# Attention inside a hybrid encoder layer: v in groups of eight columns, and TensorE's transposes in longer runs

## The chip, the cores and the metric

The kernel runs on one core of one Trainium2 chip. The metric is the device time of one execution in microseconds (us). Before the change three runs gave a median of 1982.31 us (1982.19 to 1984.06).

## The reference

The layer works on 512 tokens of width 2048, which lie on a grid of 8 rows and 64 columns. All numbers are float32. One input projection is split between two groups. Group A is a convolution module with a LayerNorm. Group B is attention: 16 heads of 64 numbers, and each query sees all 8 rows and a window of 16 columns, clamped at the grid's edge. Both results are normalised, put side by side, projected, and added to x; a gated MLP with a short convolution and a last norm follow.

```python
proj = einsum("bsd,dc->bsc", rms_norm(x, attn_norm_g), w_in)   # u_val, u_gate, q, k, v
# attention, for a row r of the grid; col_idx[c] = 16 columns around c, clamped to the grid
k_win = k_rows[:, :, col_idx];  v_win = v_rows[:, :, col_idx]
scores = einsum("bchd,bicjhd->bchij", q_row * 64**-0.5, k_win) + bias     # rows i, columns j
p = softmax(scores over (i, j))
out = einsum("bchij,bicjhd->bchd", p, v_win)
# the rest of the layer
mixed = concat(rms_norm(y_conv), rms_norm(y_na))
x = x + mixed @ w_out
up = depthwise_conv(rms_norm(x) @ w_up, width 3);  gate, val = split(up)
x = x + (silu(gate) * val) @ w_down
return rms_norm(x)
```

## The kernel before, in words

**Matmuls of the weights.** Weights come in units of 128 x 1024 numbers. `parts` (L128) splits each into a high part `whi` on ScalarE (L131) and a low part `wlo` on VectorE (L132), and `group` (L144) runs 24 matmuls on it: eight pairs of high parts (L148 and L149) and then eight with the low part (L151). `weights` (L170) prepares three units ahead, and there are four buffers for each part. An input projection of 128 output columns is two units (`project`, L335). `ORDER` says which projections come when: "a" is group A's, "q" is q, k and v of a pair of heads.

**Attention in steps.** The sixteen heads are worked on as eight pairs. `qkv(p)` (L437) projects q, k and v of a pair, transposed, with the channels of the two heads on the 128 partitions and the 512 tokens along the free axis. `attend(p, ...)` (L459) is a generator. After every unit of weights `tick` (L156) lets the next step of the oldest unfinished generator be issued behind the unit's last matmul; a second list, `asteps`, does the same for group A's norms (`group_a`, L398), which begin with pair 5. Each `yield` is the end of a step. The steps of a pair are:

- load the two halves of the bias table, and transpose v (L467, tile `trv`, ScalarE's copies `vt` at L469);
- scores (L478, tile `sc`) of four blocks of 16 columns, each against 32 columns of keys, for both heads, and the softmax of each half (L488 to L496, tile `s`);
- one empty step;
- `turn` of the first half (L506, tile `trp`; ScalarE's copies `pt` at L511), eight transposes, a copy behind each four;
- `turn` of the second half;
- values (L520, tile `po`), and behind them the copy `ao` (L554) and its split.

Block b of the queries uses the columns from `KC0[b]` = 0, 8, 24, 32 on, 32 of them in 8 rows, so 256 keys. For v, `qkv` writes these four windows out, one behind the other (L454), and as they overlap, 1024 columns stand where there are 512 tokens. So v takes eight transposes of 128 x 128.

**PSUM.** Eight banks: three for projections (`mm`), two for the tag `sc`, two for `tr`, one for `po`. The scores and the probabilities' transposes use `sc` and `tr`, v's transposes `tr`, the values `po`, and the norms' sums (`stat`, L223) the first bank of `sc`. Both halves of a tile under `sc` are one tile to the scheduler.

**Order.** A scheduler orders each engine's instructions by priority and by its own estimate of when they are ready. `pin` (keep_in_program_order) ties an instruction of TensorE to the one issued before it. `shifted(-SOONER)` gives the copies `pt` an earlier priority. Behind the input projections comes `out_half` (L581): sixteen units with group A's part, which also still carry the last steps of attention, and sixteen with attention's part. All of the MLP follows it.

Of the kernel before, what the change touches and what calls it, by code (L numbers as in the profile page):

```python
# [10 lines left out]
F32 = mybir.dt.float32  # L11
F32R = mybir.dt.float32r
AF = mybir.ActivationFunctionType
# [3 lines left out]
P = 128  # L17
D = 2048
S = 512
GW = 64  # L20
CONV = 1024
HEADS = 16
DH = 64
NA = 1024
CK = 31
WH = 8
# [7 lines left out]
NF = FF // P  # L34
U = 8
PAD = CK // 2
KW = 32
BLK = 16
NB = GW // BLK
KC0 = [0, 8, 24, 32]  # L40
H = S // 2
NK = NF // 2
KEEP = 4
# [15 lines left out]
ROW = 2048  # L59
ORDER = "aaaqqaqaaaqqaqqq"  # L60
NORM_AT = 5
RA_AFTER = 5

PCOLS = [("g1", KD), ("dww", NC_ * CK), ("dwb", NC_), ("lng", NC_), ("lnb", NC_), ("cog", NC_),
# [10 lines left out]
def layer(ctx: ExitStack, tc: tile.TileContext, xT, xn, w_0, w_in, w_out, w_up, w_down, par, tab, g3, out):  # L75
    nc = tc.nc
# [6 lines left out]
    psa = ctx.enter_context(tc.tile_pool(name="psa", bufs=1, space=bass.MemoryType.PSUM))  # L83
# [9 lines left out]
    def t2(name, dt=F32):  # L93
        return tp.tile([P, S], dt, tag="t2k", name=name)
# [86 lines left out]
    sums = {}  # L181
# [48 lines left out]
    def root_steps(sums, n, name):  # L230
# [17 lines left out]
        ps = stat()  # L248
# [3 lines left out]
        nc.scalar.activation(res, ps, AF.Copy)  # L252
        return res

    def rsqrt_steps(acc, n, name):
# [4 lines left out]
        return (yield from root_steps(ps[:, :S // P], n, name))  # L260


    xs, x1 = [], []
    pin = tc.keep_in_program_order
# [33 lines left out]
    for u in range(2):  # L298
        raw, i = raw_unit(w_in[NC_ + 1, :, u * U * P:(u + 1) * U * P], U * P)
# [15 lines left out]
    for step in ORDER:  # L315
        i = next(a_ if step == "a" else q_)
# [7 lines left out]
    rstd, late = [], []  # L324
# [71 lines left out]
    ma, ra = [], []  # L396

    def group_a():  # L398
        yield
        while taps:  # L400
            yield
        acc = t2("acc")
        nc.vector.tensor_add(acc, ys[0], ys[1])
        for i in range(2, NC_):
            nc.vector.tensor_add(acc, acc, ys[i])
        yield
        ps = psa.tile([P, 2, S], F32, tag="sc", name="st")[:, 0]
        nc.tensor.matmul(ps, ones, acc, start=True, stop=True)
        mu = t2("mu")
        nc.vector.tensor_scalar(mu, ps, 1.0 / CONV, None, op0=ALU.mult)  # L410
        acc = t2("acc")
        for i in range(NC_):
            nc.vector.tensor_sub(ys[i], ys[i], mu)
            sum_sq(acc, ys[i], i == 0)
        yield
        yield
        r = yield from rsqrt_steps(acc, CONV, "rln")
        acc = t2("acc")
        for i in range(NC_):
            nc.vector.tensor_mul(ys[i], ys[i], r)  # L420
            nc.scalar.activation(ys[i], ys[i], AF.Silu, scale=pc("lng", i), bias=pc("lnb", i))
            ma.append(split(ys[i], pc("cog", i), "ma"))
        for i in range(NC_):
            sum_sq(acc, ys[i], i == 0)
        for _ in range(RA_AFTER):
            yield

        ra.append((yield from rsqrt_steps(acc, CONV, "ra")))


    mb, rb = [], []
# [2 lines left out]
    def grid(t, c0, w):  # L434
        return t.rearrange("p (r c) -> p r c", c=GW)[:, :, c0:c0 + w]

    def qkv(p):  # L437
        got = []
        for j, nm in enumerate("qkv"):
            ps = project(2 * NC_ + j * NP_ + p)  # L440
            if nm == "q":

                t = t2(nm)
                by = "p (r b c) -> p r b c"
                nc.vector.tensor_mul(t.rearrange("p (b r c) -> p r b c", b=NB, r=WH),
                                     ps.rearrange(by, b=NB, r=WH), rstd[0].rearrange(by, b=NB, r=WH))
            elif nm == "k":
                t = t2(nm)
                nc.vector.tensor_mul(t, ps, rstd[0])
            else:  # L450

                t = [t2("vw").rearrange("p (b k) -> p b k", b=2) for _ in range(NB // 2)]
                for b in range(NB):
                    nc.vector.tensor_mul(t[b // 2][:, b % 2].rearrange("p (r c) -> p r c", c=KW), grid(ps, KC0[b], KW),  # L454
                                         grid(rstd[0], KC0[b], KW))
            got.append(t)
        return got

    def attend(p, q, k, v):  # L459


        hps = [slice(j * DH, (j + 1) * DH) for j in range(2)]
        vt = []
        for half in range(2):
            ps = psa.tile([P, 4, P], F32, tag="tr", name="trv", bufs=2)
            for c in range(4):
                nc.tensor.transpose(ps[:, c, :], v[half][:, c // 2, c % 2 * P:(c % 2 + 1) * P], ident)  # L467
            t = t2("vt").rearrange("p (c k) -> p c k", c=4)
            nc.scalar.activation(t, ps, AF.Copy)  # L469
            vt.append(t)  # L470
        po = psa.tile([P, S], F32, tag="po", name="po")
        soft = []

        def scores(b0, both, more=False):
            for i in range(2):
                b = b0 + i
                for j, hp in enumerate(hps):
                    m = nc.tensor.matmul(both[j][:, i, :], q[hp, b * P:(b + 1) * P], grid(k, KC0[b], KW)[hp],  # L478
                                         start=True, stop=True)
                    if more or i or j:  # L480
                        pin(m)
# [19 lines left out]
        def turn(two, more=False):  # L501
            for j in range(2):
                s, ps = soft.pop(0), two[j]
                for i in range(2):
                    for ch in range(2):
                        m = nc.tensor.transpose(ps[:, 2 * i + ch, :], s[:, i, ch * P:(ch + 1) * P], ident)  # L506
                        if more or i or j or ch:
                            pin(m)
                pt = t2("pt").rearrange("p (c k) -> p c k", c=4)
                with shifted(-SOONER):  # L510
                    nc.scalar.activation(pt, ps, AF.Copy)  # L511
                pts.append(pt)

        def values(b0, more=False):
            for i in range(2):
                b = b0 + i
                for ch in range(2):
                    for j in (1, 0):
                        hp = hps[j]
                        m = nc.tensor.matmul(grid(po, b * BLK, BLK)[hp], vt[b // 2][:, 2 * (b % 2) + ch, hp],  # L520
                                             pts[b0 + j][:, 2 * i + ch, :], start=(ch == 0), stop=(ch == 1))
                        if more or (i, ch, j) != (0, 0, 1):
                            pin(m)
# [13 lines left out]
        both = psa.tile([P, 2, 2, 2 * P], F32, tag="sc", name="sc")  # L537
        both = [both[:, j] for j in range(2)]
        more = [psa.tile([P, 2, 2 * P], F32, tag="tr", name="sc", bufs=2) for _ in range(2)]
        scores(0, both)  # L540
        scores(2, more, True)
        softmax(both)
        softmax(more)
        yield
        yield
        both = psa.tile([P, 2, 4, P], F32, tag="sc", name="trp")
        turn([both[:, j] for j in range(2)])
        yield
# [508 lines left out]
```

## Time and profile before

| what | value |
|---|---|
| median of three runs | 1982.31 us |
| profiled execution | 1981.86 us |
| its span, first to last instruction | 1980.1 us |
| TensorE busy | 1965.8 us, 99% |
| VectorE busy | 1617.2 us, 82% |
| ScalarE busy | 1098.3 us, 55% |
| TensorE's granted clock, mean | 0.998 |

The profile comes from one execution. "PE" is TensorE, "DVE" VectorE, "ACT" ScalarE, "SPq" the queue of SyncE, which issues loads; "L148" is line 148 of the kernel. A row of the timeline has the start in us, the duration in us (of the whole group, where like instructions follow each other), the engine, the line, the operation, output <- input, shapes and the count (x8). What stands in brackets is how long the engine sat idle before it, and who ended that. Matmuls overlap in a pipeline, so the step from one start to the next counts, not the duration. A scores matmul leaves two records, a transpose one.

### The profile page before, as it was taken

To read this page: it belongs to the slowest core of one execution; us is meant where nothing else is said; L and a number is where in the kernel's file an instruction comes from. 1 tells how busy PE (TensorE), PEld (TensorE's weight loads), DVE (VectorE), ACT (ScalarE), POOL (GpSimd) and SP (SyncE) were. 2 spreads that over 40 slices of the span, in tenths; PEclk is the share of its full clock that TensorE was granted. 3 is DMA by queue.
4 is the path that set the end of the run, shared out by engine and by line. 5 is a ranking of instruction groups with operands and counts; after the bars stand their busy time and mean duration, and the time that the engine had idled before them with its cause. 6 is when DMAs were issued, how large, how long until landed. Compare 5 with 4: busy or idle time off the path is not lost.

```text
span 1980.1 us, 27714 instructions
## 1 busy us (share of the span) xinstructions
PE 1965.8 (99%) x10173; PEld 1668.0 (84%) x10173; DVE 1617.2 (82%) x2362; ACT 1098.3 (55%) x1726; POOL 226.0 (11%) x310
## 2 busy tenths in 40 slices
PE   9999999999999999999999999999999999999998
PEld 7888888888788888888888888888888888888886
DVE  5987688788557888988888898989898898886765
ACT  7244424438525676666666666666666644554654
POOL 0111111111001111111111111111110400000000
PEclk9999999999999999999999999999999999999999
DMA  9776776776858889999999999999986977666663
GB/s 368 191 194 179 185 184 184 187 186 186 271 149 202 218 225 271 242 271 242 269 243 267 260 246 264 249 268 245 271 221 184 366 249 230 221 216 194 192 197 122
DMA packets 141817, 450.98 MB, mean 228 GB/s; under 512 B 15088, under 2 KB 23536, under 8 KB 140272
## 3 DMA queue, kind: packets, MB, share of 16 engines
q1 hardware_dynamic: 88880, 293.46, 44.3%
q0 software_dynamic: 42624, 148.92, 35.3%
q10 hardware_dynamic: 10176, 6.83, 1.1%
q8 instruction: 80, 1.31, 0.3%
q14 instruction: 57, 0.47, 0.1%
HBM read 430.27 MB, written 111.15 MB: 273 GB/s over the span
## 4 chain that ended last, share of the span: by engine, by line
PE 93%; ACT 2%; DVE 2%; DMA 1%; issue 1%; ACTq 0%; SPq 0%; DVEq 0%
PE pu L728 43%; PE pd L867 21%; PE pj L151 6%; PE pj L148 6%; PE pj L149 6%; PE po L148 3%; PE po L151 3%; PE po L149 3%; PE po L520 1%; PE trp L506 1%; ACT s L496 1%; PE pj L364 1%; DMA x<-in_xT 1%; DVE s L488 1%; ACT s L493 0%
## 5 line engine op out<-in xcount | busy, mean ns | idle before, releaser
L131 ACT ACTIVATE whi<-raw 128x1024 fp32r<-128x1024 f32 x573 | 605.1, 1057 | 573.1 <-PE pj L149 176.1
L132 DVE TENSOR_TENSOR wlo<-raw,whi 128x1024 fp32r<-128x1024 f32 x573 | 699.5, 1221 | 235.5 <-ACT whi L131 192.1
L728 PE MATMUL pu<-xc,whi 128*128 128x512 f32 x2464 | 593.6, 391 | 0.0
L728 PEld LDWEIGHTS pu<-xc,whi 128*128 128x128 f32 x2464 | 451.4, 188 | 86.7 <-DVE xc L616 0.4
L728 PEld LDWEIGHTS pu<-xc,wlo 128*128 128x128 f32 x2464 | 319.2, 191 | 13.7
L728 PE MATMUL pu<-xc,wlo 128*128 128x256 f32 x2464 | 324.2, 283 | 0.0
L867 PE MATMUL pd<-whi,ho 128*128 128x512 f32 x1232 | 305.0, 389 | 0.0
L867 PEld LDWEIGHTS pd<-whi,ho 128*128 128x128 f32 x1232 | 231.1, 188 | 48.6 <-DVE vl L741 0.5
L148 PE MATMUL pj<-xh,whi 128*128 128x512 f32 x608 | 241.4, 397 | 0.0
L149 PE MATMUL pj<-xl,whi 128*128 128x512 f32 x608 | 237.4, 391 | 0.0
L390 DVE SCALAR_TENSOR_TENSOR y<-ch,prm,y 128x500 f32<-128x500 f32 (+14 forms) x240 | 177.2, 741 | 5.1
L867 PE MATMUL pd<-wlo,ho 128*128 128x512 f32 x616 | 165.1, 389 | 0.0
L151 PE MATMUL pj<-xh,wlo 128*128 128x512 f32 x608 | 151.0, 390 | 0.0
L148 PEld LDWEIGHTS pj<-xh,whi 128*128 128x128 f32 x608 | 114.2, 188 | 26.4 <-issue 3.4
L867 PEld LDWEIGHTS pd<-wlo,ho 128*128 128x128 f32 x616 | 115.6, 188 | 24.0
L151 PEld LDWEIGHTS pj<-xh,wlo 128*128 128x128 f32 x608 | 114.1, 188 | 23.6
L149 PEld LDWEIGHTS pj<-xl,whi 128*128 128x128 f32 x608 | 114.3, 188 | 23.0 <-issue 0.2
L737 ACT ACTIVATE pu<-pu 128x512 f32<-128x512 f32 x132 | 76.5, 580 | 93.2 <-PE pu L728 93.2
L677 POOL DMA_DIRECT2D raw<-in_w_up x88 | 78.0, 887 | 361.3 <-DVE wlo L132 154.1
L203 POOL DMA_DIRECT2D ws<-in_w_down x88 | 79.6, 904 | 299.4 <-DMA ws<-in_w_down 115.6
L200 POOL DMA_DIRECT2D ws<-ws x44 | 23.4, 531 | 321.6 <-PE pj L151 109.2
L200 POOL DMA_DIRECT2D ws<-in_w_down x44 | 23.1, 524 | 321.5 <-PE pj L151 178.1
(185 smaller groups left out, 1986.7 us busy)
## 6 DMA issues: line engine op xcount, KB each, us to landing
raw<-in_w_up SPq DMA_DIRECT2D x220, 512.0 KB, 5.9
ws<-in_w_down POOLq DMA_DIRECT2D x132, 512.0 KB, 6.1
raw<-in_w_up POOLq DMA_DIRECT2D x88, 512.0 KB, 7.3
raw<-ws SPq DMA_DIRECT2D x88, 512.0 KB, 3.7
raw<-in_w_in SPq DMA_DIRECT2D x76, 512.0 KB, 5.2
raw<-in_w_down SPq DMA_DIRECT2D x66, 512.0 KB, 3.9
ws<-ws POOLq DMA_DIRECT2D x44, 512.0 KB, 5.7
raw<-in_w_out SPq DMA_DIRECT2D x32, 512.0 KB, 5.0
```

The source lines that it names most:

```text
L131: i = nc.scalar.activation(hi[:, :n], raw[:, :n], AF.Copy)
L132: j = nc.vector.tensor_sub(lo[:, :n], raw[:, :n], hi[:, :n].bitcast(F32))
L148: nc.tensor.matmul(ps, hi, mh, start=first and k == 0, stop=False)
L149: nc.tensor.matmul(ps, hi, ml, start=False, stop=False)
L151: i = nc.tensor.matmul(ps, lo[:, wk * P:(wk + 1) * P], mh, start=False, stop=last and k == len(ws) - 1)
L200: behind(nc.gpsimd.dma_start(wsum[c][k], a), ins)
L203: nc.gpsimd.dma_start(wsum[c][k], w_down[k, {1: A21, 2: A11, 4: A11, 6: A12}[c]], accum_op=ALU.add, max_dma_last_dim=ROW)
L390: nc.vector.scalar_tensor_tensor(y[:, a:b], h[:, a + j - PAD:b + j - PAD], prm[:, o:o + 1], y[:, a:b], op0=ALU.mult, op1=ALU.add)
L677: nc.gpsimd.dma_start(a[c], w_up[f, q2], accum_op=ALU.add)
L728: i = nc.tensor.matmul(ps[:, :n], part[:, k * P:(k + 1) * P], comb[c][k][:, :n], start=j == 0 and not more, stop=j == 2 * U - 1, skip_grou ...
L737: nc.scalar.activation(to, ps, AF.Copy)
L867: m = nc.tensor.matmul(ps[i], h[:, o + t * P:o + (t + 1) * P], w[:, d], start=start and not more and kind == 0 and j == 0, stop=stop and k ...
```

## The change

Keys and values are kept in groups of eight columns: `qkv` writes k and v as eight groups, each of 8 rows by 8 columns (64 numbers), so two neighbouring groups are 128 numbers in one piece. A window of 32 columns is four groups. Windows 0 and 3 begin at an even group (0 and 4) and are read in place; windows 1 and 2 begin at an odd one (1 and 3). For them there is a second copy of the keys, `ks`, with the groups in the order 2, 1, 4, 3, 6, 5; ScalarE makes it with two copies of 128 x 192. `KEYS` says for every block which of the two it reads and from where, `WITHIN` in which order the groups stand there, and the bias table is laid out for that order on the host.

Now v has four transposes, into the bank `po`. ScalarE copies the result three times: whole, and for each half of the partitions (one group of a pair) three quarters, so that the groups stand in the same order as in `ks`. These transposes are issued in the step of the scores, in one pinned run with them.

All sixteen transposes of the probabilities go into one step and one run, into two banks of `sc` and two of `tr`, and the four copies `pt` are issued behind the last of them. Three steps lie from the scores to this turn, four in pairs 5 and 6 (`LATER`), and the values follow one step later. The broadcast of group A's last norm, `ra`, takes its bank from `po`.

```diff
-KW = 32
-KC0 = [0, 8, 24, 32]
+HG = 8
+KEYS = ((0, 0), (1, 0), (1, 1), (0, 2))
+WITHIN = ((0, 1, 2, 3), (1, 0, 3, 2))
+LATER = (5, 6)
...
-        ra.append((yield from rsqrt_steps(acc, CONV, "ra")))
+        ra.append((yield from rsqrt_steps(acc, CONV, "ra",
+                                          lambda: psa.tile([P, S], F32, tag="po", name="st"))))
...
-            elif nm == "k":
+            else:
                 t = t2(nm)
-                nc.vector.tensor_mul(t, ps, rstd[0])
-            else:
-                t = [t2("vw").rearrange("p (b k) -> p b k", b=2) for _ in range(NB // 2)]
-                for b in range(NB):
-                    nc.vector.tensor_mul(t[b // 2][:, b % 2].rearrange("p (r c) -> p r c", c=KW), grid(ps, KC0[b], KW),
-                                         grid(rstd[0], KC0[b], KW))
+                by = "p (r g c) -> p r g c"
+                nc.vector.tensor_mul(t.rearrange("p (g r c) -> p r g c", g=2 * NB, r=WH),
+                                     ps.rearrange(by, g=2 * NB, r=WH), rstd[0].rearrange(by, g=2 * NB, r=WH))
+            if nm == "k":
+                ks = t2("ks")
+                at = "p (n s k) -> p n s k"
+                for i, by in enumerate((slice(1, NB), slice(0, NB - 1))):
+                    nc.scalar.activation(ks.rearrange(at, s=2, k=DH)[:, :NB - 1, i], t.rearrange(at, s=2, k=DH)[:, by, i],
+                                         AF.Copy)
+                t = t, ks
...
-        vt = []
-        for half in range(2):
-            ps = psa.tile([P, 4, P], F32, tag="tr", name="trv", bufs=2)
-            for c in range(4):
-                nc.tensor.transpose(ps[:, c, :], v[half][:, c // 2, c % 2 * P:(c % 2 + 1) * P], ident)
-            t = t2("vt").rearrange("p (c k) -> p c k", c=4)
-            nc.scalar.activation(t, ps, AF.Copy)
-            vt.append(t)
-        po = psa.tile([P, S], F32, tag="po", name="po")
+        def turned_v():
+            ps = psa.tile([P, NB, P], F32, tag="po", name="trv")
+            for c in range(NB):
+                m = nc.tensor.transpose(ps[:, c, :], v[:, c * P:(c + 1) * P], ident)
+                if c:
+                    pin(m)
+            vt.extend(t2("vt").rearrange("p (c k) -> p c k", c=NB) for _ in range(2))
+            nc.scalar.activation(vt[0], ps, AF.Copy)
+            for hp, by in zip(hps, (slice(1, NB), slice(0, NB - 1))):
+                nc.scalar.activation(vt[1][hp, :NB - 1], ps[hp, by], AF.Copy)
...
-                    m = nc.tensor.matmul(both[j][:, i, :], q[hp, b * P:(b + 1) * P], grid(k, KC0[b], KW)[hp],
+                    m = nc.tensor.matmul(both[j][:, i, :], q[hp, b * P:(b + 1) * P],
+                                         ks[KEYS[b][0]][hp, KEYS[b][1] * P:][:, :2 * P],
                                          start=True, stop=True)
...
+        def turned_p(two):
+            for ps in two:
                 pt = t2("pt").rearrange("p (c k) -> p c k", c=4)
                 with shifted(-SOONER):
                     nc.scalar.activation(pt, ps, AF.Copy)
                 pts.append(pt)
...
-        scores(0, both)
+        turned_v()
+        scores(0, both, True)
         scores(2, more, True)
         softmax(both)
         softmax(more)
+        for _ in range(4 if p in LATER else 3):
+            yield
+        both = psa.tile([P, 2, 4, P], F32, tag="sc", name="trp")
+        both = [both[:, j] for j in range(2)]
+        more = [psa.tile([P, 4, P], F32, tag="tr", name="trp", bufs=2) for _ in range(2)]
+        turn(both)
+        turn(more, True)
+        turned_p(both + more)
         yield
-        yield
-        both = psa.tile([P, 2, 4, P], F32, tag="sc", name="trp")
-        turn([both[:, j] for j in range(2)])
-        yield
-        turn([psa.tile([P, 4, P], F32, tag="tr", name="trp", bufs=2) for _ in range(2)])
-        yield
-        values(0)
-        values(2, True)
+        po = psa.tile([P, S], F32, tag="po", name="po")
+        values(po, 0)
+        values(po, 2, True)
```

More of the change, by code (lines that the diff above doesn't have):

```diff
@@ L228, in layer, with root_steps @@
     where = []
-    def root_steps(sums, n, name):
+    def root_steps(sums, n, name, bank=None):
         v, r, y = (sm.tile([P, S // P], F32, tag="rs" + c, name="rs" + c) for c in "vry")
@@ L247, in root_steps @@
         yield
-        ps = stat()
+        ps = bank() if bank else stat()
         for i in range(2):
@@ L253, in root_steps, with rsqrt_steps @@
         return res
-    def rsqrt_steps(acc, n, name):
+    def rsqrt_steps(acc, n, name, bank=None):
         ps = stat()
@@ L259, in rsqrt_steps @@
             nc.tensor.matmul(ps[:, i:i + 1], acc[:, i * P:(i + 1) * P], ones[:, 0:1], start=True, stop=True)
-        return (yield from root_steps(ps[:, :S // P], n, name))
+        return (yield from root_steps(ps[:, :S // P], n, name, bank))
     xs, x1 = [], []
@@ L456, in qkv, with attend @@
+            if nm == "k":
[5 more added lines that the diff above has]
+                t = t, ks
             got.append(t)
         return got
[L459 removed]
+    def attend(p, q, ks, v):
         hps = [slice(j * DH, (j + 1) * DH) for j in range(2)]
[L463 to L472 removed]
+        vt, soft = [], []
+        def turned_v():
[8 more added lines that the diff above has]
+                nc.scalar.activation(vt[1][hp, :NB - 1], ps[hp, by], AF.Copy)
@@ L512, in turn, with values @@
                 pts.append(pt)
-        def values(b0, more=False):
+        def values(po, b0, more=False):
             for i in range(2):
@@ L519, in values @@
                         hp = hps[j]
-                        m = nc.tensor.matmul(grid(po, b * BLK, BLK)[hp], vt[b // 2][:, 2 * (b % 2) + ch, hp],
+                        m = nc.tensor.matmul(grid(po, b * BLK, BLK)[hp], vt[KEYS[b][0]][:, KEYS[b][1] + ch, hp],
                                              pts[b0 + j][:, 2 * i + ch, :], start=(ch == 0), stop=(ch == 1))
@@ L1035 @@
     qr, qc = np.divmod(np.arange(P), BLK)
-    kr, kc = np.divmod(np.arange(2 * P), KW)
+    kg, kr, kc = np.unravel_index(np.arange(2 * P), (NB, WH, HG))
     tab = np.full((HEADS, 3, P, 2 * P), NEG, rpb.dtype)
@@ L1039 @@
         c = b * BLK + qc[:, None]
-        k = KC0[b] + kc[None, :]
+        swapped, at = KEYS[b]
+        k = ((2 * at + swapped + np.array(WITHIN[swapped])[kg]) * HG + kc)[None, :]
         start = np.clip(c - WW // 2, 0, GW - WW)
```

## The prediction

> **What bounds the kernel now.** I read the page first: shares of busy time, the granted clock, the chain that ended last.
>
> ```profile
> PE 1965.8 (99%) x10173; PEld 1668.0 (84%) x10173; DVE 1617.2 (82%) x2362; ACT 1098.3 (55%) x1726; POOL 226.0 (11%) x310
> ...
> PEclk9999999999999999999999999999999999999999
> ...
> PE 93%; ACT 2%; DVE 2%; DMA 1%; issue 1%; ACTq 0%; SPq 0%; DVEq 0%
> ```
>
> TensorE is busy 99% of the span at full clock and is 93% of the chain. So an instruction less on TensorE, or a wait less, should come off the end, unless it opens a gap. Next I read TensorE's timeline where pairs of heads are worked on. A unit is 24 projection matmuls, and its last eight (L151) make one row; from one such row to the next is one unit with what is put in between.
>
> ```profile
> 104.55 1.98 PE L151 MATMUL pj<-xh,wlo 128*128 128x512 f32 x8
> ...
> 109.99 1.98 PE L151 MATMUL pj<-xh,wlo 128*128 128x512 f32 x8
> 111.81 1.03 PE L467 MATMUL trv<-ident,vw 128*128 128x128 f32 x8
> ...
> 116.34 1.98 PE L151 MATMUL pj<-xh,wlo 128*128 128x512 f32 x8
> 118.25 2.00 PE L478 MATMUL sc<-k,q 64*128 64x256 f32 x16
> ...
> 123.97 1.98 PE L151 MATMUL pj<-xh,wlo 128*128 128x512 f32 x8
> ...
> 169.52 1.98 PE L151 MATMUL pj<-xh,wlo 128*128 128x512 f32 x8
> 171.34 0.60 PE L506 MATMUL trp<-ident,s 128*128 128x128 f32 x4
> ...
> 172.71 0.60 PE L506 MATMUL trp<-ident,s 128*128 128x128 f32 x4
> ...
> 175.92 1.98 PE L151 MATMUL pj<-xh,wlo 128*128 128x512 f32 x8
> 177.74 1.03 PE L506 MATMUL trp<-ident,s 128*128 128x128 f32 x8
> ...
> 182.27 1.97 PE L151 MATMUL pj<-xh,wlo 128*128 128x512 f32 x8
> 184.17 1.97 PE L520 MATMUL po<-pt,vt 128*64 128x128 f32 x32
> ...
> 189.83 1.98 PE L151 MATMUL pj<-xh,wlo 128*128 128x512 f32 x8
> ...
> 460.50 1.98 PE L151 MATMUL pj<-xh,wlo 128*128 128x512 f32 x8
> ...
> 544.90 1.98 PE L151 MATMUL po<-mah,wlo 128*128 128x512 f32 x8
> ...
> 551.29 1.98 PE L151 MATMUL po<-mah,wlo 128*128 128x512 f32 x8
> ...
> 557.24 1.98 PE L151 MATMUL po<-mah,wlo 128*128 128x512 f32 x8
> ```
>
> A unit with nothing in it takes 109.99 - 104.55 = 5.44 us. What a unit takes beyond 5.44 is the price of what was put in, drains and waits included: eight transposes of v 6.35 - 5.44 = 0.91; the scores 7.63 - 5.44 = 2.19; two runs of four transposes of the probabilities 6.40 - 5.44 = 0.96, so 0.48 a run; a run of eight 6.35 - 5.44 = 0.91; the values 7.56 - 5.44 = 2.12. From 4 to 8 transposes is 0.43, so one costs 0.107 and a run 0.05 on top.
>
> The whole stretch, by groups of instructions between its first and last row:
>
> ```profile
> L151 PE MATMUL pj<-xh,wlo 128*128 128x512 f32 x496 | 123.3, 390 | 0.0
> ...
> L151 PE MATMUL po<-mah,wlo 128*128 128x512 f32 x64 | 15.8, 389 | 0.0
> ```
>
> 560 such matmuls are 70 units, 380.8 us. From 109.99 to 557.24 are 447.25, so 66.45 us were put in. Of these the three norms, which the change only moves, take about 5.3: each 0.95 for its sums (544.90 to 551.29) and 0.5 for its broadcast (551.29 to 557.24), and some 0.95 for the mean's matmul, which I put at the price of the sums. Attention costs 61.1 us, 7.6 a pair, where the prices above make 0.91 + 2.19 + 0.96 + 0.91 + 2.12 = 7.09. The rest is waits:
>
> ```profile
> 129.41 1.98 PE L151 MATMUL pj<-xh,wlo 128*128 128x512 f32 x8
> ...
> 132.93 0.66 PE L506 MATMUL trp<-ident,s 128*128 128x128 f32 x4 [0.16 <-ACT pt L511]
> 136.19 1.98 PE L151 MATMUL pj<-xh,wlo 128*128 128x512 f32 x8
> ...
> 518.01 2.00 PE L478 MATMUL sc<-k,q 64*128 64x256 f32 x16 [0.79 <-ACT ra L252]
> ```
>
> In the first pair the two runs of four cost 6.78 - 5.44 = 1.34: the second waits for ScalarE's copy of the first, since both write one tile. Pairs 6 and 7 (counted from 0), which share the engines with group A's norms, are worst: 460.50 to 544.90 is 84.40 us for 12 units (65.28), so 19.12 put in, 17.2 without norms.
>
> **The change, part by part.**
>
> *v's transposes.* Four for eight, 32 fewer in all, in one run ahead of the scores. Four cost 0.43 to 0.48 by the rows above, depending on whether the run's 0.05 is shared with the scores. I take 0.45, so v and scores make 2.64 where they made 3.10. The scores' matmuls keep number and shape, and a keys' operand that lies in one piece of 256 columns, not eight of 32, I give no gain: 16 in 1.92 us is 0.12 for 256 columns, in proportion with the projections' 5.44/24 = 0.227 for 512. The scores start at 118.25, 0.10 behind the eight L151 that began at 116.34 (8 x 0.227 = 1.81). [...]
>
> *The probabilities' transposes.* Sixteen in one run: 16 x 0.107 + 0.05 = 1.77, where two runs of four and one of eight took 1.87 without waits and 2.2 with them. All four copies come behind, so no transpose waits for a copy.
>
> *The values.* Unchanged, 2.12. A pair now costs 2.64 + 1.77 + 2.12 = 6.53, eight 52.2.
>
> *ScalarE and VectorE.*
>
> ```profile
> L454 DVE TENSOR_TENSOR vw<-pj,rstd x32: 410/415/425, 106.6 to 506.7; 128x256 f32<-128x256 f32 x32
> ...
> L445 DVE TENSOR_TENSOR q<-pj,rstd x8: 679/682/691, 85.7 to 490.2; 128x512 f32<-128x512 f32 x8
> ...
> L469 ACT ACTIVATE vt<-trv x16: 576/596/599, 112.4 to 516.9; 128x512 f32<-128x512 f32 x16
> ...
> 130.55 0.90 ACT L496 ACTIVATE s<-s,su 128x256 f32<-128x256 f32 x2
> ...
> 110.19 1.06 ACT L131 ACTIVATE whi<-raw 128x1024 fp32r<-128x1024 f32 x1 [4.38 <-PE pj L149]
> ```
>
> VectorE's four multiplies for v (4 x 0.415) become one like q's (0.68; at worst the old 1.66), and k's stays one. ScalarE gets two copies of 128x192 for the shifted keys (nearest row: two of 128x256 in 0.90, so 0.5 to 0.9 together) and three copies of v for two (0.596 each; the two of 64x384 between 0.45 and 0.6): 0.8 to 1.5 us a pair more. ScalarE waits 4.38 us a unit for TensorE to give a weight buffer back, and that covers it. Without that cover, in pairs 5 to 7, the weights are still split some three units (16 us) ahead. I cost both at nothing.
>
> *Turn and values one tick apart.* The turn moves behind three units, not two, and for pairs 5 and 6 behind four; values stay a tick behind it, at the place of before for pairs 0 to 4 and 7. The scores at 118.25 had their last scaled probability at 130.55 + 0.90 = 131.45; the turn came at 129.41 + 1.81 = 131.22, in part ahead of that, and one unit later is 136.66, 5.2 us behind it. Queued behind the turn on TensorE is everything, so this slack matters; the added ScalarE work (1.5) doesn't use it up. The four copies take 4 x 0.5 us from the run's first quarter on, a unit ahead of the values.
>
> *Where a wait appears.* In the changed program's order on ScalarE the four copies stand right behind the turn in seven pairs. In pair 6 they stand behind three weight splits, the last of which waits for the unit directly ahead of the values, and the copy of `ra`, which now uses the values' bank, is behind them. The same shape is in the trace:
>
> ```profile
> 515.25 1.98 PE L151 MATMUL po<-mah,wlo 128*128 128x512 f32 x8
> ...
> 515.45 1.06 ACT L131 ACTIVATE whi<-raw 128x1024 fp32r<-128x1024 f32 x1 [4.38 <-PE po L149]
> 516.41 1.06 ACT L469 ACTIVATE vt<-trv 128x512 f32<-128x512 f32 x2
> 517.36 0.60 ACT L252 ACTIVATE ra<-st 128x512 f32<-128x512 f32 x1
> ```
>
> There a split, two copies and `ra` ended at 517.96 and the scores waited 0.79. With four copies it is 0.95 longer (516.41 to 517.36 is two), a wait of about 1.8 us at pair 6's values. `ra` read in pair 7's scores (0.79) goes. The wait is bounded by 0 and the 3.7 us that this ScalarE run takes.
>
> *SyncE.* One load of w_out is moved behind the sixteen reloads of x:
>
> ```profile
> 502.04 11.91 SPq L578 DMA_DIRECT2D x<-in_xT  x16
> 514.31 52.56 SPq L126 DMA_DIRECT2D raw<-in_w_out  x12
> ```
>
> It is the eleventh of w_out, goes out some 12 us later, and its unit starts ten units (54 us) behind the first of that projection. Cost: nothing. POOL's queue keeps its order.
>
> *Sum.* 61.1 - 52.2 - 1.8 = 7.1 us. The profiled execution took 1981.86 (span 1980.1), so 1974.8; the median of the three runs, 1982.31, is 0.45 above it, so **1975.2 us**. Own range: 1973.0 (no wait in pair 6, 0.05 shared) to 1977.2 (2 us of further waits where group A's norms now fall between turn and values).
>
> **Rivals.**
>
> *Pairs 6 and 7 give nothing.* Their 17.2 us hold ScalarE and VectorE work of the norms; if that sets the pace there, transposes saved turn into waits. Then pairs 0 to 5 alone count: 61.1 - 17.2 = 43.9, less 6 x 6.53 = 39.2, leaves 4.7: 1977.6, and with 2 us of new waits 1979.6. For it: the waits of 0.79 and in pair 6. Against: the turn of pair 6 gets a unit or two more time.
>
> *Better.* No wait in pair 6 and none at the norms: 1973.0 or a little less.
>
> *Slower: the softmax chain misses the single turn.* A run of sixteen waits for the last of four softmaxes, where four transposes could start on the first. The chain took 13.2 us (118.25 to 131.45) and has 18.4 (to 136.66). It decides from there: for slower by 4 us every pair would have to wait (7.1 + 4)/8 = 1.4 us, a chain of 19.8, half as long again; at 19.9 it gives 1982.3 + 4 + 8 x 0.1, some 1987. Only 1.5 us of work is added.
>
> *The clock.* The granted clock could fall in the longer transposes' run. In the run of eight it didn't:
>
> ```profile
> 138.00:138.80 0.80, 0.80 (x10) 0.79 (x8) 0.77 (x2) 0.16 (x1) 0.33 (x1) 1.00 1.05 361
> ```
>
> If it halved for the unit behind each run, that is 8 x 5.44 = 43.5: 2018.7. [...]
>
> **How the numbers follow.** Under 0.2%, 4 us, nothing can be told from no change: faster is below 1978.3. Forecast 0.66; pairs 6 and 7 give nothing 0.16, half of it faster; better 0.10; slower by the chain 0.05, by the clock 0.02; 0.01 for no gain at all. Faster 0.66 + 0.08 + 0.10, less 0.01 of the forecast's edge, 0.83; same 0.10; slower 0.07. The range takes in better and most of the second case: 1972.4 to 1979.6.
>
> **What would show it.** Right: unit to unit 5.44 + 2.6 with v and scores, + 1.8 with the sixteen, + 2.1 with the values; 32 records fewer of v's transposes; no wait of `trp` for `pt`; one wait of `po` for ScalarE in pair 6 near 1.8 us; everything behind it shifted by about 7. Wrong: waits of `trp` for `s` in several pairs, of `st` or `sc` for ScalarE around the norms beyond 2 us, or a granted clock under 1 in the runs.

## The result and the profile after

The changed kernel takes **1976.01 us** (median of six runs, 1975.79 to 1977.32); beside it the kernel before took 1982.18 us (six runs, 1982.03 to 1984.06). The ratio is 0.997, with a 95% interval of 0.996 to 0.998: 6.2 us faster. The profiled execution took 1976.0 us, its span 1974.2. The forecast was 1975.2.

The page of the changed kernel: shares of busy time, granted clock, chain that ended last.

```profile
PE 1960.6 (99%) x10141; PEld 1668.0 (84%) x10141; DVE 1611.7 (82%) x2338; ACT 1105.8 (56%) x1750; POOL 225.7 (11%) x310
...
PEclk9999999999999999999999999999999999999999
...
PE 98%; DVE 1%; ACT 0%; DMA 0%; issue 0%; ACTq 0%; DVEq 0%
```

TensorE is still the bound, with 32 instructions less, and its share of the chain went from 93% to 98%: the short waits for ScalarE and VectorE along the way are nearly gone. TensorE's timeline in the first pair of heads (the last eight matmuls of a unit are L153 now):

```profile
110.36 1.98 PE L153 MATMUL pj<-xh,wlo 128*128 128x512 f32 x8
115.80 1.98 PE L153 MATMUL pj<-xh,wlo 128*128 128x512 f32 x8
117.61 0.60 PE L476 MATMUL trv<-ident,v 128*128 128x128 f32 x4
118.14 0.70 PE L488 MATMUL sc<-k,q 64*128 64x256 f32 x4
...
123.87 1.98 PE L153 MATMUL pj<-xh,wlo 128*128 128x512 f32 x8
...
134.75 1.98 PE L153 MATMUL pj<-xh,wlo 128*128 128x512 f32 x8
136.57 1.91 PE L517 MATMUL trp<-ident,s 128*128 128x128 f32 x16
141.98 1.98 PE L153 MATMUL pj<-xh,wlo 128*128 128x512 f32 x8
143.89 1.97 PE L534 MATMUL po<-pt,vt 128*64 128x128 f32 x32
149.54 1.98 PE L153 MATMUL pj<-xh,wlo 128*128 128x512 f32 x8
```

An empty unit is 5.44 us as before (110.36 to 115.80). v and the scores add 8.07 - 5.44 = 2.63 (2.60 in most other pairs), the sixteen transposes 7.23 - 5.44 = 1.79 (1.78 to 1.80 in the others), the values 7.56 - 5.44 = 2.12. The waits of TensorE, in the view of waits, of the changed kernel (the two rows left out lie in its first 13 us):

```profile
PE po L534 <- ACT ra L254: 1.9, 1, 1.9
...
PE st L410 <- DVE acc L407: 0.3, 1, 0.3
```

No transpose waits for a copy or for a softmax any more. One long wait is left in attention. It stands in pair 6 (TensorE, then ScalarE, both from the timeline):

```profile
495.22 1.91 PE L517 MATMUL trp<-ident,s 128*128 128x128 f32 x16
...
506.51 1.98 PE L153 MATMUL po<-mah,wlo 128*128 128x512 f32 x8
510.40 1.97 PE L534 MATMUL po<-pt,vt 128*64 128x128 f32 x32 [1.92 <-ACT ra L254]
516.06 1.98 PE L153 MATMUL po<-mah,wlo 128*128 128x512 f32 x8
```

```profile
501.27 1.06 ACT L133 ACTIVATE whi<-raw 128x1024 fp32r<-128x1024 f32 x1 [5.96 <-PE po L151]
506.71 1.06 ACT L133 ACTIVATE whi<-raw 128x1024 fp32r<-128x1024 f32 x1 [4.38 <-PE po L151]
507.79 2.06 ACT L525 ACTIVATE pt<-trp 128x512 f32<-128x512 f32 x4
509.72 0.63 ACT L254 ACTIVATE ra<-st 128x512 f32<-128x512 f32 x1
```

The transposes of this pair ended at about 497.1, and ScalarE was idle for 5.96 us up to 501.27 and for 4.38 us up to 506.71, but the four copies stand behind two weight splits that wait for TensorE to give buffers back. So the copies start only at 507.79 and `ra` ends at 510.35.

From the row at 110.36 to the last row of the stretch, at 562.12, lie 72 units: 451.76 - 391.68 = 60.08 us were put in, where it was 66.45. That is 6.37 less. The kernel's end moved by 5.9 (spans 1980.1 and 1974.2), because the stretch itself began later: its first such row is at 99.48, where it is at 99.11 in the kernel before, and at 99.02 and 98.98 in other kernels below, whose work up to there is the same.

### The profile page after: what moved, and what is told of

Its sections match the earlier page's. It is cut to its first block, busy times and chain, and to the rows that moved or that the text cites. A ratio compares the mean times of both kernels' runs of the same rounds, so it can differ in the third digit from the quotient of the medians.

```text
span 1974.2 us, 27655 instructions
## 1 busy us (share of the span) xinstructions
PE 1960.6 (99%) x10141; PEld 1668.0 (84%) x10141; DVE 1611.7 (82%) x2338; ACT 1105.8 (56%) x1750; POOL 225.7 (11%) x310
## 4 chain that ended last, share of the span: by engine, by line
PE 98%; DVE 1%; ACT 0%; DMA 0%; issue 0%; ACTq 0%; DVEq 0%
PE pu L746 43%; PE pd L885 21%; PE pj L150 7%; PE pj L151 7%; PE pj L153 7%; PE po L150 3%; PE po L151 3%; PE po L153 3%; PE po L534 1%; PE sc L488 1%; PE trp L517 1%; PE pj L366 1%; DMA we<-in_w 0%; PE trx L641 0%; PE pj L370 0%; DVE acc L407 0%
## 5 line engine op out<-in xcount | busy, mean ns | idle before, releaser
L153 PE MATMUL pj<-xh,wlo 128*128 128x512 f32 x608 | 150.3, 389 | 0.0
L153 PEld LDWEIGHTS pj<-xh,wlo 128*128 128x128 f32 x608 | 114.1, 188 | 23.7
```

The lines of the kernel that those rows point to most:

```text
L153: i = nc.tensor.matmul(ps, lo[:, wk * P:(wk + 1) * P], mh, start=False, stop=last and k == len(ws) - 1)
```

## The experiments

The theory: (a) fewer and longer runs of transposes save their own time on TensorE, and a later turn saves the waits; (b) pair 6's new wait comes from the order on ScalarE alone. Rivals: the copies' place at the end of the run matters; pairs 6 and 7 limit the gain whatever the order; long runs cost clock.

"Put in" is the stretch's inserted work, worked out as above.

| kernel | us, median (range, runs) | put in, us | wait at pair 6's values, us |
|---|---|---|---|
| changed kernel | 1976.01 (1975.79 to 1977.32, 6) | 60.08 | 1.92 |
| v_only | 1979.6 (1979.15 to 1980.04, 11) | 63.73 | none |
| turn_only | 1979.82 (1979.39 to 1980.01, 11) | 64.23 | none |
| follow6 | 1973.55 (1973.41 to 1974.18, 5) | 58.03 | none |
| nolater | 1973.39 (1973.28 to 1973.55, 4) | 58.08 | none |
| inline | 1975.19 (1974.82 to 1975.41, 6) | 59.47 | 1.28 |
| follow_inline | 1974.87 (1974.68 to 1975.21, 5) | 59.32 | 1.28 |
| early | 1977.07 (1) | 61.71 | none |
| apart | 1978.68 (1977.12 to 1978.98, 10) | 61.36 | 1.92 |
| apart_again | 1977.63 (1976.84 to 1978.86, 11) | 62.90 | 1.92 |
| double | 1987.28 (1) | 71.65 | none |
| wait3 | 1979.04 (1978.54 to 1979.70, 11) | 63.21 | 3.53 |
| wait2 | 1976.35 (1975.37 to 1977.09, 8) | 61.61 | 1.92 |

The kernel before, measured beside these experiments, had medians of 1981.73 to 1981.85, where it had 1982.18 beside the changed kernel. So the changed kernel's time stands 0.3 to 0.45 us too high against theirs, and below a gain is counted from the kernel before that was measured with it: 6.2 us for the changed kernel. Put in, from the profiles, is the second measure.

**v_only: v and the keys alone.** Turn in two steps, each copy behind its four transposes, as before.

```diff
-        for _ in range(4 if p in LATER else 3):
-            yield
...
-        turn(both)
-        turn(more, True)
-        turned_p(both + more)
+        yield
+        yield
+        both = psa.tile([P, 2, 4, P], F32, tag="sc", name="trp")
+        turn([both[:, j] for j in range(2)])
+        yield
+        turn([psa.tile([P, 4, P], F32, tag="tr", name="trp", bufs=2) for _ in range(2)])
```

v's transposes also got back their own step and bank, and `ra` its bank.

> The part for v and the keys alone: four transposes of v for eight (own run, in the first step, in a bank of tr), the keys' second copy, the scores' new operands; turns, copies and ra's bank as before the change. Theory (each instruction on TensorE counts in full): eight pairs save 0.43 to 0.48 each, 3.4 to 3.9 us, so 1978.3 to 1978.8; the run of four costs 0.48, the scores stay at 2.19, and the waits of trp for pt (1.2 us) stay. Rival (the gain is the waits that the turn's new form takes away, and v's transposes lay beside other work): 1982.0 us.

Ratio to before 0.9989 (0.998 to 0.9998). TensorE's timeline of v_only, in the first pair and in pair 7:

```profile
110.16 1.98 PE L153 MATMUL pj<-xh,wlo 128*128 128x512 f32 x8
111.98 0.60 PE L475 MATMUL trv<-ident,v 128*128 128x128 f32 x4
116.07 1.98 PE L153 MATMUL pj<-xh,wlo 128*128 128x512 f32 x8
...
132.80 0.66 PE L516 MATMUL trp<-ident,s 128*128 128x128 f32 x4 [0.31 <-ACT pt L521]
...
515.92 0.70 PE L487 MATMUL sc<-k,q 64*128 64x256 f32 x4 [1.30 <-ACT ra L254]
```

Four transposes cost 5.91 - 5.44 = 0.47 against 0.91, eight times 0.44 = 3.5. Put in is only 2.72 less: the waits of before stayed and some grew (0.16 to 0.31 in the first pair, 0.79 to 1.30 ahead of pair 7's scores). The expectation had left that growth out and was a microsecond too low.

**turn_only: the single later turn alone.** v as in the kernel before, eight transposes from the overlapping windows; the rest of the change is kept.

```diff
-            else:
-                t = t2(nm)
-                by = "p (r g c) -> p r g c"
...
+            elif nm == "k":
+                t = t2(nm)
+                nc.vector.tensor_mul(t, ps, rstd[0])
+            else:
+                t = [t2("vw").rearrange("p (b k) -> p b k", b=2) for _ in range(NB // 2)]
...
```

> The turn alone: sixteen transposes of the probabilities in one run with the four copies behind them, later steps for pairs 5 and 6, ra in the values' bank; v with eight transposes in the first step and the keys as before the change. Theory: pairs cost 0.91 + 2.19 + 1.79 + 2.12 = 7.01, 56.1 in all against 61.1, less the new wait in pair 6 (about 1.9) and 0.6 at the norms, so 2.5 us faster than before, 1979.7. Rival (the waits are nearly all of the gain): 1977 us or less.

Ratio 0.9989 (0.9981 to 0.9998), and the time is the one expected (the gain, 2.0, is 0.5 less than expected). The turn takes 1.77 to 1.80, as in the full change, and no turn waits for a copy. Pair 6's late copies are felt a little earlier: pair 7's transposes of v, which come directly ahead of pair 6's values, wait 0.79 us for them. The two parts make 2.72 + 2.22 = 4.94 of the 6.37; together they save 1.4 more. Some of it is the joined run (apart, below), and some are waits that only one part leaves: 1.03 ahead of the mean's matmul and the 0.79 in turn_only, those of v_only above. I have not taken this remainder apart to the last tenth.

**follow6: one edge of order.** The weight split that is issued next after pair 6's turn is pinned behind its four copies (the middle lines stand in `parts`, after the instruction that makes `whi`).

```diff
-    tight, taps = [], []
+    tight, taps, follow = [], [], []
...
+        if follow:
+            pin(i)
+            follow.pop()
...
         turned_p(both + more)
+        if p == 6:
+            follow.append(1)
```

> The changed kernel with one edge more: in pair 6 the weight split that is issued next after the turn may not go ahead of the four copies pt on ScalarE, so the copies and ra come ahead of three splits and not behind them. Nothing else moves. Theory (the wait of 1.92 us at pair 6's values comes from ScalarE's order alone): the wait goes, values 4.11 becomes about 2.12, 1974.1 us. Rival (ScalarE has too much to do there, and the wait only moves): another wait of about 2 us appears at the weights or at pair 7, 1976.0 us.

Ratio 0.9959 (0.9946 to 0.9971): 8.3 us faster than the kernel before, 2.1 more than the changed kernel's 6.2. The intervals of the two ratios overlap, but no execution of one kernel comes within 1.6 us of the other's, and put in falls by 2.05. ScalarE's timeline and then TensorE's, of follow6, in pair 6:

```profile
495.78 2.06 ACT L528 ACTIVATE pt<-trp 128x512 f32<-128x512 f32 x4 [1.94 <-PE trp L520]
497.71 0.63 ACT L257 ACTIVATE ra<-st 128x512 f32<-128x512 f32 x1
498.19 1.09 ACT L133 ACTIVATE whi<-raw 128x1024 fp32r<-128x1024 f32 x1
```

```profile
505.99 1.98 PE L156 MATMUL po<-mah,wlo 128*128 128x512 f32 x8
507.90 1.97 PE L537 MATMUL po<-pt,vt 128*64 128x128 f32 x32
513.55 1.98 PE L156 MATMUL po<-mah,wlo 128*128 128x512 f32 x8
```

The same copies now start 12 us earlier, the values cost 2.12 with no wait, and nothing else became late. So (b) holds.

**nolater: three steps in pairs 5 and 6 too.** This undoes one line of the change.

```diff
-LATER = (5, 6)
+LATER = ()
```

> The changed kernel with three steps, not four, between scores and turn in pairs 5 and 6 as in the others (LATER empty). If the fourth step is needed because group A's norms delay the softmaxes there, transposes of these two pairs wait for s or the run breaks in two, and the time is 1976.5 to 1978 us. If the wait at pair 6's values came only from the weight splits ahead of the copies, an earlier turn gives another order on ScalarE without that wait, and the time is 1974 to 1975.

Ratio 0.9958 (0.9944 to 0.9971), 8.35 us faster than the kernel before, as follow6 within noise, and below even the better of the two expectations. With the turn one step earlier the scheduler places pair 6's copies with the softmax, ahead of the splits. Of TensorE's timeline of nolater, the turn and values of pair 6:

```profile
480.75 1.98 PE L153 MATMUL pj<-xh,wlo 128*128 128x512 f32 x8
483.93 0.76 PE L517 MATMUL trp<-ident,s 128*128 128x128 f32 x4
...
496.80 1.98 PE L153 MATMUL po<-mah,wlo 128*128 128x512 f32 x8
```

The sixteen transposes fall apart into short runs between projection matmuls, and yet two units with the turn, the values and a norm's sums take 16.05 us, 5.17 put in, where 1.79 + 2.12 + 0.95 = 4.86 would be the price in whole runs. The fourth step keeps the run whole (0.3 us) and costs the wait (2.0).

**inline and follow_inline: each copy behind its four transposes.** The change in inline, and follow_inline has the edge of follow6 beside it:

```diff
-
-        def turned_p(two):
-            for ps in two:
                 pt = t2("pt").rearrange("p (c k) -> p c k", c=4)
...
-        turned_p(both + more)
```

> The changed kernel with the four copies not at the run's end but each behind its four transposes, as before the change. Theory (two halves of a tile under sc are one tile to the scheduler, so the second four wait for the copy of the first): the run of sixteen falls apart, four transposes in one place and twelve a few matmuls later, 0.05 us a run more and waits of trp for pt of 0.2 to 0.7 us in several pairs, 2 to 4 us in all: 1978 to 1980. Rival (the copies' place is of no account once the turn comes a unit later): 1976.0 us, no waits.

> The order edge of pair 6 and each copy behind its four transposes, together. If the copies' place matters only through ScalarE's order in pair 6, the edge has already taken that wait and nothing is left to gain: the time with the edge alone, 1973.5 us, within 1 us. If copies that start earlier are worth something by themselves, both gains add up: 1973.5 less the 0.8 us that the early copies alone gave, 1972.7 or below.

Inline was not slower: it gained 6.5 us on the kernel before, 0.4 more than the changed kernel, and 0.61 less is put in. TensorE's timeline of inline, in the first pair and in pair 6:

```profile
136.24 0.60 PE L517 MATMUL trp<-ident,s 128*128 128x128 f32 x4
...
137.60 1.47 PE L517 MATMUL trp<-ident,s 128*128 128x128 f32 x12
...
506.67 1.53 PE L517 MATMUL trp<-ident,s 128*128 128x128 f32 x12
509.49 1.97 PE L531 MATMUL po<-pt,vt 128*64 128x128 f32 x32 [1.28 <-ACT ra L254]
```

The scheduler puts four projection matmuls between the first four transposes and the other twelve, and the pair still pays 1.80 to 1.84. In pair 6 the twelve come two units (12 us) behind the first four, directly ahead of the values, so three copies and `ra` are waited for, 1.28; with it pair 6's turn, norm and values cost 0.42 less than in the changed kernel. The sums behind pair 5's turn cost 0.27 less. Those two make up the gain. In follow_inline, ScalarE's timeline:

```profile
507.40 1.57 ACT L525 ACTIVATE pt<-trp 128x512 f32<-128x512 f32 x3 [11.24 <-PE trp L520]
...
509.33 2.97 ACT L133 ACTIVATE whi<-raw 128x1024 fp32r<-128x1024 f32 x3
```

The edge holds, the splits come behind the copies, but the copies themselves wait for the twelve late transposes. The wait stays at 1.28, and both theories on record for this kernel were wrong. So the copies' place at the end of the run is worth 0.01 to 0.04 us a pair. Only with the edge in pair 6 does more hang on it: there the run stays whole and early, and follow6 has 1.29 less put in than follow_inline.

**early: the turn two steps behind the scores, in all pairs.**

```diff
-        for _ in range(4 if p in LATER else 3):
+        for _ in range(2):
```

> The changed kernel with the turn two steps after the scores in every pair, not three or four. It measures the slack of the softmax chain. Theory (chain of about 13.2 us from the first score to the last probability; two units and the scores give 13.0, and the sixteenth transpose only comes 1.8 later): the last transposes wait 0 to 0.6 us in pairs 0 to 5, more in 6 and 7, where the norms are, 3 us or more each: 1978 to 1984 us. Rival (the chain has slack, and the extra unit buys nothing): 1976 us or less.

One run, 1977.07, between the two expectations. In pairs 0 to 4 the run of sixteen comes one unit earlier, still costs 1.79 to 1.80 and waits for nothing; the 1.63 us more that are put in lie in pairs 5 to 7, by the norms (0.60 for a copy, 0.40 and 0.44 for softmaxes, runs broken up). The softmax chain had more room than the prediction counted: in the first pair ScalarE finishes the last probability at 131.63, the run starts at 130.76, and only its last four transposes, by their price 1.3 us into the run, need it.

**apart and apart_again: v's transposes in a run of their own**, one step ahead of the scores. The second is the first once more.

```diff
+        turned_v()
...
-        turned_v()
-        scores(0, both, True)
+        scores(0, both)
```

> The changed kernel with v's four transposes in a run of their own one step ahead of the scores, not joined with them. It gives the price of joining. Theory (a run has 0.05 us of its own): unit with four transposes 0.48, with the scores 2.17 to 2.19, together 2.65 to 2.67 for 2.60, 0.4 us in all: 1976.4. Rival (each change between projections and other matmuls costs TensorE 0.2 or more): 1977.6 or more.

> The kernel with v's four transposes in a run of their own, a second time. Its inserted work was 1.28 us more than that of the changed kernel, its time about 2.7 more. If the rest was chance (the first weight loads, a wait in the MLP), it is 1977.3 within 0.5 us this time and TensorE does not wait for xc in the MLP; if the rest belongs to this order of work, it is again above 1978.3 with that wait.

The four transposes cost 0.48 and the scores 2.19 to 2.20, together 2.67, joined 2.60: joining is worth 0.07 a pair, half a microsecond, as the theory had it, though the time is that of the rival. The mean's matmul also waited longer (1.02 against 0.26), and put in grew by 1.28. But the executions of the two runs together lie in two groups: 10 of the 21 between 1976.84 and 1977.98, and 11 between 1978.33 and 1978.98. The profile of apart (1977.98) is of the first, that of apart_again (1978.33) of the second. The view by windows of 2 us, 512 to 516, after the wait of 1.92 in pair 6; the third column from the end is the granted clock. First apart, then apart_again:

```profile
512.00:514.00 2.00, 2.00 (x30) 1.76 (x27) 0.91 (x2) 0.43 (x1) 0.00 (x0) 1.00 1.03 398
514.00:516.00 2.00, 2.00 (x12) 1.66 (x11) 1.05 (x2) 1.97 (x5) 0.00 (x0) 1.00 1.04 422
```

```profile
512.00:514.00 2.00, 2.00 (x21) 1.67 (x16) 0.43 (x1) 0.24 (x1) 0.00 (x0) 0.53 1.04 419
514.00:516.00 2.00, 2.00 (x9) 1.52 (x9) 0.85 (x2) 1.60 (x3) 0.00 (x0) 0.62 1.03 416
```

Same program, same wait: in one execution the clock stayed, in the other it fell, and put in is 1.54 more. That was in no theory so far, and a wait of 0.5 us in the MLP (`pu` for `xc`) that apart had, and that I had suspected, is not in apart_again, whose profiled execution is the longer one.

**wait3 and wait2: pair 6's wait made longer.** In wait3 all four copies of pair 6 are made twice, in wait2 only the last (with `and len(pts) == 3` in the condition):

```diff
                     nc.scalar.activation(pt, ps, AF.Copy)
+                    if p == 6:
+                        nc.scalar.activation(pt, ps, AF.Copy)
```

> Each of the four copies pt of pair 6 is made twice, so that the wait at pair 6's values grows by four copies, from 1.9 to about 3.9 us; nothing else is changed. If a wait costs its own length and no more, the time is 1976.0 + 2.0 = 1978.0 us and the granted clock stays at 1.00 in pair 6. If an idle TensorE can lose its clock, as in one of the two profiles with v's transposes apart (0.53 and 0.62 behind a wait of 1.92 us), the longer wait makes that the rule: the clock shows below 1 behind it and the time is 1.5 us more, 1979.5, in most executions.

> Only the last copy pt of pair 6 is made twice; it comes behind ra, and the values' second half waits for it, about 0.5 us more idle time in pair 6, 2.4 us in all. If a wait costs its own length: 1976.5 us in all executions. If the clock can fall behind it, the executions lie in two groups, near 1976.5 and near 1978.

wait3, TensorE's timeline and the windows:

```profile
511.94 3.58 PE L536 MATMUL po<-pt,vt 128*64 128x128 f32 x32 [3.53 <-ACT ra L254]
```

```profile
512.00:514.00 2.00, 2.00 (x20) 2.00 (x22) 1.30 (x2) 0.38 (x1) 0.00 (x0) 0.52 1.02 418
514.00:516.00 2.00, 2.00 (x18) 1.61 (x15) 0.00 (x0) 0.44 (x1) 0.00 (x0) 0.62 0.84 336
```

The wait grew by 1.61, and put in by 3.13: the fall of the clock adds 1.5. All eleven executions are at 1978.5 or above, 1979.04 in the median where the theory of a falling clock had 1979.5 and the other 1978.0; both had been counted from 1976.0, some 0.35 too high beside the kernel before as it was measured with wait3 (1981.83, against 1982.18). In wait2 the doubled copy came behind `ra` and did not lengthen the wait (1.92), but its executions again fall in two groups, 1975.37 to 1975.82 and 1976.88 to 1977.09, four each, and the profiled one, 1976.96, has the fall (0.62 and 0.53 from 510 to 514): its values, which start at 509.81, take 3.09 us, where they take 1.97 in the changed kernel. The mean granted clock on record for every execution goes with the groups: in wait2 0.999 in the four short ones, 0.997 or 0.998 in the four long ones; in apart and apart_again 0.999 in nine of the ten short ones, 0.997 or 0.998 in all eleven long ones; in wait3 0.997 or 0.998 in all eleven. So behind a wait of 1.92 us the clock fell in some executions, and behind one of 3.53 in the profiled one and, by times and mean clocks, in the others. The mean clock alone decides nothing, as executions without such a loss also come out at 0.998.

**double: every transpose of the probabilities twice**, in runs of 32.

```diff
-                        m = nc.tensor.transpose(ps[:, 2 * i + ch, :], s[:, i, ch * P:(ch + 1) * P], ident)
-                        if more or i or j or ch:
-                            pin(m)
+                        for again in range(2):
+                            m = nc.tensor.transpose(ps[:, 2 * i + ch, :], s[:, i, ch * P:(ch + 1) * P], ident)
+                            if more or i or j or ch or again:
+                                pin(m)
```

> The changed kernel with every transpose of the probabilities done twice, one right behind the other, into the same place: runs of 32. It gives the price of a transpose on the path and shows the clock over a longer run. Theory: 128 transposes more at 0.107 are 13.7 us, the run costs 0.05 + 32 x 0.107 = 3.5, granted clock 1.00; in pair 6 the order on ScalarE is another one and the wait is smaller, by up to 1.9: 1987.8 to 1989.7 us. Rival (the granted clock falls in long runs of transposes): clock below 1 in the runs or behind them, units of more than 5.44, 2000 us and more.

TensorE's timeline of double, and a window of it:

```profile
134.55 1.98 PE L153 MATMUL pj<-xh,wlo 128*128 128x512 f32 x8
...
143.52 1.98 PE L153 MATMUL pj<-xh,wlo 128*128 128x512 f32 x8
```

```profile
138.00:140.00 2.00, 2.00 (x20) 2.00 (x19) 2.00 (x3) 1.58 (x3) 0.00 (x0) 1.00 1.01 404
```

A run of 32 costs 8.97 - 5.44 = 3.53, so (3.53 - 1.79)/16 = 0.109 a transpose, at a granted clock of 1.00; the unit behind it takes 7.56 with the values, as in the changed kernel. The one run is 0.5 us below the expected range, about as much as the kernel before was lower beside it (1981.73, against 1982.18).

## Why the prediction was right, point by point

The gain was 6.2 us where the prediction had 7.1, and the profiled execution 1976.0 where it had 1974.8. By its steps:

- **v's transposes.** 2.64 foreseen, 2.60 to 2.63 measured. The choice that the run's 0.05 is shared with the scores holds: joined 2.60, apart 2.67. The prediction means its prices with drains included, but no run shows a drain by itself; what the runs show beside the transposes' own time is the 0.05 of a run (0.48 for four in apart, less 4 x 0.107) and the 0.07 a pair that joining saves.
- **The probabilities' transposes.** 1.77 foreseen, 1.78 to 1.80 measured. That no transpose waits for a copy came true, but the reason given isn't the only way to it: inline has the copies where they were and has no such wait either, as four projection matmuls, 4 x 0.227 = 0.91 us, stand where the first copy, some 0.52 (four take 2.06), is made. What of the later turn lets the scheduler do so was not tested.
- **The values.** 2.12, as foreseen. With the norms' parts taken out, attention costs 52.2 us without pair 6's wait, the number foreseen.
- **The wait in pair 6.** Foreseen 1.8 with its cause, measured 1.92 (4.11 - 2.12 = 1.99 put in). follow6 and nolater show the cause. What the prediction didn't see is that the extra step, which it counted as room for pair 6, is itself what put the copies behind the splits: without it the kernel gains 2.2 us more, and put in is 2.00 less.
- **The norms.** Here lies the largest miss: the step that took them as only moved, at 5.3. In the changed kernel they cost 5.9. The mean's matmul (one, of 512 columns, which leaves two records) had been put at 0.95. In the kernel before, that is about right: its unit takes 7.71 - 5.44 = 2.27 together with two runs of four and a wait of 0.20, which make some 1.37 by the first pair's 1.34 with a wait of 0.16, so an estimated 0.9 is left. First the kernel before, then the changed one:

```profile
437.92 1.98 PE L151 MATMUL pj<-xh,wlo 128*128 128x512 f32 x8
...
441.47 0.66 PE L506 MATMUL trp<-ident,s 128*128 128x128 f32 x4 [0.20 <-ACT pt L511]
442.90 1.04 PE L408 MATMUL st<-acc,ones 128*128 128x512 f32 x2
...
445.63 1.99 PE L151 MATMUL pj<-xh,wlo 128*128 128x512 f32 x8
```

```profile
433.90 1.97 PE L153 MATMUL pj<-xh,wlo 128*128 128x512 f32 x8
436.14 1.10 PE L410 MATMUL st<-acc,ones 128*128 128x512 f32 x2 [0.26 <-DVE acc L407]
440.74 1.98 PE L153 MATMUL pj<-xh,wlo 128*128 128x512 f32 x8
```

  In the changed kernel it stands alone between projection matmuls, behind a wait, and costs 1.40. Next, the sums that follow pair 5's turn in the same step cost 3.03 - 1.79 = 1.24. Their tile lies in the first bank of `sc`, which two of the four copies must read out first; inline, where the copies start earlier, pays 0.95 for these sums, which fits a wait for that bank, though no row names it. The two broadcasts behind a turn or the values cost 0.44 each, not 0.5. In sum 0.6 more than assumed. With pair 6 (0.2) and the start of the stretch (0.37 later) this makes the 1.2 us between 1974.8 and 1976.0.
- **ScalarE and VectorE.** ScalarE's busy time rose by 7.5 us, 0.94 a pair, inside the 0.8 to 1.5 foreseen; VectorE's fell by 5.5. No wait of TensorE for the keys or for v appears, so the cost of nothing holds. Nor does one for the moved load of w_out.
- **The rivals.** Pairs 6 and 7 do give something: 15.0 us without norms where it was 17.2, and that with pair 6's wait. Follow6 shows that "better", a gain of 9.3, was within 1.0 us of the 8.3 that an unspoilt order reaches. The softmax chain misses nothing in pairs 0 to 4 even a step earlier (early). The granted clock stays at 1.00 in and behind the run of sixteen (changed kernel, 136 to 144) and the run of 32 (double, 134 to 144), both of the first pair; the halving that the prediction reckons with is its author's assumption, and none of these windows shows one.

## What to carry to other kernels

Where a scheduler sets a queue's order, read in the trace what stands ahead of each late instruction: here four copies, whose input was there at about 497.1 and which started at 507.79, stood behind two weight splits that waited for buffers, and one edge of order, or one step less, gained a third as much again as the whole change had (2.1 or 2.2 against 6.2 us). Giving a step "more room" was not free here: it moved its copies behind work that blocks, and 2.00 us more were put in. And work that a change only moves has to be priced at its new place: the norms, taken over at their old price, were the largest miss.

## What the runs showed of the hardware

In some executions a wait of TensorE of 1.92 us cost nearly twice its length. Behind it the granted clock fell to 0.53 and 0.62 in two windows of 2 us in apart_again, and stayed at 1.00 in apart; behind 3.53 us it fell to 0.52 and 0.62 in wait3. Each fall cost 1.5 us (put in 62.90 against 61.36 for the same program, so (1.92 + 1.5)/1.92 = 1.8 times the wait). The changed kernel's profile has the wait without the fall (1.00 from 510 to 516); whether its one run at 1977.32 had it stays open: that run has no profile, and its mean clock, 0.998, two of the shorter runs show too. What makes the same wait lose the clock at one time and not at another, no run here shows.
